# A hybrid attention block on one core: gate columns tied behind each DeltaNet recurrence, output transposes and gating issued after them

## The chip, the cores and the metric

The kernel runs as one program on one core of a Trainium2 chip. The metric is the device time in microseconds (us) of one execution. The kernel before takes 3041.43 us, the median of three runs (3039.56, 3041.43 and 3043.84). One further execution was profiled; every row shown here comes from it.

## The reference

One transformer block with a context: 1024 tokens of width 1024, 256 context tokens, 8 heads. An input projection feeds two mixers, a differential attention and a gated DeltaNet; their outputs are merged under two sigmoid gates and followed by an MLP. All is f32. The part that matters here is the DeltaNet, cut to its core:

```python
qkv = silu(depthwise_conv_centred(concat([p[3], p[4], p[5]]), conv_w))   # 7 taps
q, k, v = split(qkv);  q = l2_normalize(q) * 128**-0.5;  k = l2_normalize(k)
# per head and direction, in chunks of the sequence
t_mat = triangular_solve(eye + a_mat, eye)          # a_mat from k k^T, beta, decay
def step(state, xs):
    v_new = u_i - w_i @ state
    o_i = q_i @ state + qk_i @ v_new
    state = state * g_i + k_i^T @ v_new
out_x = rms_norm(ox_f + flip(ox_b), norm_g) * silu(z)                    # forward + backward
# later: y = sigmoid(p[11]) * (o_da @ w_br_da) + sigmoid(p[12]) * (o_dn @ w_br_dn)
```

`p[3]`, `p[4]`, `p[5]`, `p[6]` are the q, k, v and z projections of the DeltaNet, `p[11]` and `p[12]` the columns of the two merge gates, all of them products of the input with columns of one weight.

## The kernel before

**Projections.** One projection of a head makes 128 columns for 1024 tokens. The weight's eight pieces of 128 x 128 come by DMA on SyncE's queue (line 146), ScalarE casts each to a high part `whi` (149), GpSimd makes the low part `wlo` (150), and `gemm_cols` runs three matmuls to each accumulation step (`uh·whi`, `ul·whi`, `uh·wlo`, lines 164 to 166) into the PSUM tile `pg`: 8 pieces x 3 x 2 halves of 512 tokens = 48 matmuls. The q, k and v projections (`dn_proj`) are evicted into `cvraw` (429) and convolved: ScalarE makes the middle tap, VectorE six more in each of two halves (440), ScalarE the silu (442). The z projection (`dn_gate`) needs no convolution: ScalarE evicts it with silu straight into `sz` (455), of which there is one buffer.

**A head.** `dn_prep` works ahead for the next head: it transposes k (486) and q (493), takes their norms (497), makes the decays (465 to 470), the matrices `cm` (520, 523) and `pm` (528, 530), and inverts blocks of 32 by a long list of VectorE instructions in `slX`, `slY` and `slL` (540 to 582), which go to DRAM and back (`xd`, `yd`, loads at 596 and 599). `dn_pre` transposes v and k for the head itself (646, 653). `dn_double` (611 to 634) extends the inverse from 32 to 128 rows, and `dn_chain` runs the recurrence over ten chunks in both directions: per step and direction `k·S` (676), `xs` on VectorE (678), `cm·xs` (680), scalings on ScalarE (683, 686), `k·ws` (688), the new state `S` on VectorE (693), and for the eight chunks of x the outputs (698 to 707) summed in `oacc`. After the last step the head's norm is taken (712 to 719), `oacc` is transposed by TensorE (723: eight 128 x 128 transposes into two PSUM tiles `po`), VectorE multiplies by the norm weight and by `sz` (725), and SyncE stores 512 KB to `odn_d` (727).

**Fillers.** The columns of the two merge gates are 16 projections of 128 columns (`fill_setup`). `fill(n)` issues the next n of them: 48 matmuls, an eviction on ScalarE (747), a store on SyncE (748). What is left of them, and the first attention head's columns (`fill_head`), come after the last head's recurrence.

**What sets the order.** Instructions are traced in the order of the source and then scheduled in one list by the framework, from the dependencies, a model of the costs and a priority; `self.rank(...)` sets the priority of a block. The recurrence and, in this kernel, the output transposes have the first rank (`R_CHAIN` = 0), preparation and inverse follow (`R_PREP`, `R_INV`), then the convolutions (`R_CONV`). Fillers and projections take their place in source order behind these, so `ORD` decides which of them lies next to which part. Each engine then executes its own list in order. In `dn_phase` a head's recurrence is traced, then v of the next head, k and q of the one after, two sets of gate columns, and z of the next head.

Of the kernel before, what the change touches and what calls it, by code (L numbers as in the profile page):

```python
# [32 lines left out]
W2 = (5, 5)  # L33
NB = 6
BK = (1, 1, 2, 2)
ORD = 'vkqffz'
GAP = 8
SPLIT = 508
W1 = (2, 4)
# [14 lines left out]
class K:  # L54
# [602 lines left out]
    def dn_chain(self, h, r):  # L657

        nc, dw, ds = self.nc, self.dw, self.ds
        qT, kT, vtok, pm, sz, ktok, rq, b2, bdl, cm = (  # L660
            r[x] for x in ("q", "k", "vtok", "pm", "z", "ktok", "rq", "b2", "bdl", "cm"))
        ch = lambda a, c: a[:, c * P:(c + 1) * P]
        oacc = dw.tile([P, NX, P], F32, name="oacc", bufs=1)
        order = (list(range(NT)), [1, 0] + list(range(NT - 1, NC0 - 1, -1)))
# [2 lines left out]
        for step in range(NT):  # L667
            for d in range(2):
                c = order[d][step]
                last = step == NT - 1  # L670
                S0 = S[d]
                pc = self.pc.tile([P, 3, P], F32, name=f"pc{d}")
                if S0 is None:
                    xs = vtok[:, c]
                else:
                    nc.tensor.matmul(pc[:, 0], lhsT=self.ck(kT, c), rhs=S0, start=True, stop=True)
                    xs = ds.tile([P, P], F32, name=f"xs{d}", bufs=1)
                    nc.vector.scalar_tensor_tensor(out=xs, in0=pc[:, 0], scalar=self.necg[:, d, c, h:h + 1], in1=vtok[:, c],
                                                   op0=ALU.mult, op1=ALU.add)
                nc.tensor.matmul(pc[:, 1], lhsT=cm[d][:, c], rhs=xs, start=True, stop=True)  # L680
                if not last:
                    ws = ds.tile([P, P], F32, name=f"ws{d}", bufs=1)
                    nc.scalar.activation(out=ws, in_=pc[:, 1], func=AF.Copy, scale=bdl[d][:, c:c + 1])
# [33 lines left out]
        so = self.rsqrt(ds, so, NX, "so")  # L717
        nc.vector.tensor_tensor(out=so, in0=so, in1=rq, op=ALU.mult)
        nc.vector.tensor_tensor(out=oacc, in0=oacc, in1=so.unsqueeze(2).to_broadcast((P, NX, P)), op=ALU.mult)
        for q in range(2):  # L720
            pt = self.po.tile([P, 4, P], F32, name="po")
            for c in range(4):
                nc.tensor.transpose(out=pt[:, c], in_=oacc[:, 4 * q + c], identity=self.ident)
            szq = sz[:, 512 * q:512 * q + 512]
            nc.vector.scalar_tensor_tensor(out=szq, in0=pt.rearrange("p a b -> p (a b)"), scalar=self.dng, in1=szq,
                                           op0=ALU.mult, op1=ALU.mult)
# [800 lines left out]
    def dn_phase(self):  # L1527
        tc = self.tc
        R = [{} for _ in range(H + 2)]

        def proj(h, *names):
            for nm in names:
                if h < H:
                    self.dn_gate(h, R[h]) if nm == "z" else self.dn_proj(h, nm, R[h])

        proj(0, "k", "q")
        with self.rank(R_PREP):
            self.dn_prep(0, R[0])
        proj(0, "v")
        proj(1, "k", "q")  # L1540
        proj(0, "z")
        for h in range(H):
            with self.rank(R_PREP):
                self.dn_pre(h, R[h])
            if h + 1 < H:
                with self.rank(R_PREP):
                    self.dn_prep(h + 1, R[h + 1])
            with self.rank(R_CHAIN):
                self.dn_double(h, R[h])
                self.dn_chain(h, R[h])  # L1550
            if h == H - 1:
                self.fill(100)
                self.fill_head()
            for c in ORD:
                if c == "f":
                    self.fill(1)
                else:
                    proj(h + (2 if c in "kq" else 1), c)
        self.ranks_off()


# [36 lines left out]
```

## Time and profile before

| | |
|---|---|
| median of three runs | 3041.43 us |
| profiled execution | 3038.64 us (span 3036.9) |
| TensorE matmul busy | 2828.2 us (93%), 15928 matmuls |
| VectorE | 2008.3 us (66%) |
| ScalarE | 1333.1 us (44%) |
| GpSimd | 656.6 us (22%) |
| granted TensorE clock, mean | 0.958 |
| DeltaNet heads | about 320 to 1296 us |
| first attention score (line 877) | 1350.9 us |

The shares are means over stages with different limits, so the windows of a single stage say more. Matmuls overlap each other, and the listed time of one is longer than the distance to the next. In the text below a *recurrence* is the stretch from a head's first doubling matmul to its last chain matmul, a *gap* the stretch from there to the next head's first doubling matmul. Recurrences of heads 0 to 7 are, rounded: 320 to 399, 445 to 515, 578 to 646, 687 to 767, 838 to 903, 963 to 1038, 1097 to 1165 and 1211 to 1285 us.

### The profile page before, as it was taken

The numbers are of one execution on the slowest core, as the hardware profiler recorded it, in microseconds if no ns is written. First come the engines' busy times: TensorE is split into PE (matmuls) and PEld (weight loads), VectorE is DVE, ScalarE is ACT, GpSimd is POOL, SyncE is SP. The second block draws the span as 40 slices with busy tenths as digits, with TensorE's granted clock in tenths as the row PEclk, the third lists the DMA queues.
The fourth block names the chain that finished last, engine by engine and source line by source line (L and its number), as shares of the span: only waits on it lengthen the run. The fifth ranks groups of instructions, "written<-read, shape, count | busy, mean of one in ns | idle before, by whom it ended". The sixth has DMA issues, their size and how long they took to land. (4 is left out here: it accounts for less than half of the span.)

```text
span 3036.9 us, 44469 instructions
## 1 busy us (share of the span) xinstructions
PE 2828.2 (93%) x15928; PEld 2273.6 (75%) x15928; DVE 2008.3 (66%) x3675; ACT 1333.1 (44%) x3269; POOL 656.6 (22%) x756
## 2 busy tenths in 40 slices
PE   7998989899898999989999999899999999989998
PEld 4886768677686777868887778677777677768887
DVE  4768497794967767247777778664486776544435
ACT  4655244444443544326655556564465422322210
POOL 1234223532423241021111110101001643100000
PEclk9999799998998999789999999999999999999999
DMA  7631211211212122173433332416564544453321
GB/s 253 190 110 43 52 48 34 67 53 41 70 33 66 34 63 67 37 186 81 105 93 93 91 88 66 91 39 198 158 220 131 164 143 120 137 194 104 104 63 63
DMA packets 340973, 303.09 MB, mean 100 GB/s; under 512 B 87892, under 2 KB 287700, under 8 KB 339728
## 3 DMA queue, kind: packets, MB, share of 16 engines
q1 hardware_dynamic: 318864, 252.14, 28.5%
q10 hardware_dynamic: 18304, 37.41, 4.8%
q0 software_dynamic: 3584, 10.71, 1.0%
q8 instruction: 125, 2.05, 0.3%
q14 instruction: 96, 0.79, 0.1%
HBM read 212.08 MB, written 66.06 MB: 92 GB/s over the span
## 5 line engine op out<-in xcount | busy, mean ns | idle before, releaser
L150 POOL TENSOR_TENSOR wlo<-wraw,whi 128x256 fp32r<-128x256 f32 x312 | 320.7, 1033 | 1219.5 <-ACT whi L149 987.3
L164 PE MATMUL pg<-uh,whi 128*128 128x512 f32 x1152 | 481.7, 418 | 6.6 <-ACT whi L149 3.2
L166 PE MATMUL pg<-uh,wlo 128*128 128x512 f32 x1152 | 481.3, 418 | 6.1 <-POOL wlo L150 5.8
L165 PE MATMUL pg<-ul,whi 128*128 128x512 f32 x1152 | 481.4, 418 | 0.0
L149 ACT CAST whi<-wraw 128x256 fp32r<-128x256 f32 (+1 forms) x568 | 241.0, 430 | 322.9 <-PE pg L165 102.9
L166 PEld LDWEIGHTS pg<-uh,wlo 128*128 128x128 f32 x1152 | 224.6, 195 | 49.9 <-POOL wlo L150 11.1
L164 PEld LDWEIGHTS pg<-uh,whi 128*128 128x128 f32 x1152 | 224.9, 195 | 47.0 <-ACT whi L149 4.8
L165 PEld LDWEIGHTS pg<-ul,whi 128*128 128x128 f32 x1152 | 224.8, 195 | 39.6
L1370 PE MATMUL pa<-B,A 128*128 128x512 f32 x768 | 220.6, 395 | 13.6 <-ACT B L1318 5.0
L1370 PE MATMUL pg<-B,A 128*128 128x512 f32 x768 | 219.5, 393 | 0.0
L150 DVE TENSOR_TENSOR wlo<-wraw,whi 128x256 fp32r<-128x256 f32 (+1 forms) x256 | 136.6, 542 | 120.8 <-ACT whi L149 119.1
L888 DVE TENSOR_REDUCE mp<-sx 128x1 f32<-128x1024 f32 x128 | 155.7, 1218 | 49.8 <-PE sx L878 49.4
L1370 PEld LDWEIGHTS pa<-B,A 128*128 128x128 f32 x768 | 145.9, 190 | 46.9 <-ACT B L1318 5.4
L1370 PEld LDWEIGHTS pg<-B,A 128*128 128x128 f32 x768 | 146.2, 190 | 30.7
L893 ACT ACTIVATE p<-sx,mx 128x1024 f32<-128x1024 f32 x128 | 143.2, 1118 | 53.2 <-DVE mx L889 41.9
L916 PEld LDWEIGHTS pat<-V,aT 128*128 128x128 f32 x1280 | 151.0, 193 | 14.6 <-ACT aT L914 12.1
L916 PE MATMUL pat<-V,aT 128*128 128x128 f32 x1280 | 158.8, 279 | 0.0
L913 PE MATMUL pat<-ident,p 128*128 128x128 f32 x640 | 119.6, 285 | 8.0 <-ACT oh L917 5.0
L1386 DVE TENSOR_TENSOR acc<-pa,acc 128x512 f32<-128x512 f32 x32 | 22.1, 690 | 157.0 <-PE pa L1370 157.0
L1318 ACT CAST A<-araw 128x1024 fp32r<-128x1024 f32 x32 | 33.6, 1052 | 209.7 <-PE pg L1370 171.8
L913 PEld LDWEIGHTS pat<-ident,p 128*128 128x128 f32 x640 | 74.6, 142 | 56.2 <-ACT aT L914 21.3
L877 PE MATMUL sx<-K,Q 128*128 128x512 f32 x256 | 109.5, 428 | 2.9 <-DMA wraw<-in_w_in_dram 2.0
(457 smaller groups left out, 6701.8 us busy)
## 6 DMA issues: line engine op xcount, KB each, us to landing
wraw<-in_w_in_dram SPq DMA_DIRECT2D x288, 128.0 KB
wraw<-in_w_in_dram SPq DMA_DIRECT2D x64, 256.0 KB
uraw<-in_w_mlp_dram SPq DMA_DIRECT2D x32, 512.0 KB
braw<-in_w_mlp_dram SPq DMA_DIRECT2D x32, 512.0 KB
araw<-ff_d SPq DMA_DIRECT2D x32, 512.0 KB
ff_d<-ue SPq DMA_DIRECT2D x52, 256.0 KB
adraw<-in_w_ada_dram SPq DMA_DIRECT2D x32, 320.0 KB
wa<-in_w_ada_dram SPq DMA_DIRECT2D x8, 1024.0 KB
```

What stands on the lines that cost most here:

```text
L149: nc.scalar.copy(out=hi, in_=raw)
L150: self.weng.tensor_tensor(out=lo, in0=raw, in1=hi.bitcast(F32), op=ALU.subtract)
L164: nc.tensor.matmul(o, lhsT=hi, rhs=a, start=k == 0, stop=False)
L165: nc.tensor.matmul(o, lhsT=hi, rhs=b, start=False, stop=False)
L166: nc.tensor.matmul(o, lhsT=lo, rhs=a, start=False, stop=k == KT - 1)
L877: nc.tensor.matmul(ps, lhsT=Q[m][:, qs], rhs=Kh[m][:, ks], start=True, stop=False)
L888: nc.vector.tensor_reduce(out=mp[:, m, 0:1], in_=px[m], axis=AX.X, op=ALU.max)
L893: nc.scalar.activation(out=p[:, CTX:], in_=px[m], func=AF.Exp, bias=mx[:, m:m + 1], accum_out=sp[:, 0, m:m + 1])
L913: nc.tensor.transpose(out=pt[:, c], in_=a[:, (c0 + c) * P:(c0 + c + 1) * P], identity=self.ident)
L916: nc.tensor.matmul(po, lhsT=aT[:, c], rhs=r["v"][:, c], start=c == 0, stop=c == NT - 1)
L1318: nc.scalar.copy(out=z[:, 0], in_=x)
L1370: mm = lambda x, y, **kw: nc.tensor.matmul(ps[c], lhsT=a[:, x, k], rhs=bt[:, y, s], **kw)
```

## The change

`ORD` is gone. `dn_chain` ends with the normalised `oacc`; the transposes, the gating and the store stand in a function of their own, `dn_finish`, which is traced without the first rank. After a head's recurrence v of the next head and k and q of the one after are traced, then one set of gate columns whose TensorE instructions are queued behind the head's last `cm·xs` matmul (`tc.issue_after`), then `dn_finish`, then z of the next head and a second set of gate columns. For the last head `dn_finish` is traced after all that is left of the fillers. No computation is added or left out.

```diff
--- before.py
+++ after.py
@@ -33,7 +33,6 @@
 W2 = (5, 5)
 NB = 6
 BK = (1, 1, 2, 2)
-ORD = 'vkqffz'
 GAP = 8
 SPLIT = 508
 W1 = (2, 4)
@@ -657,8 +656,8 @@
     def dn_chain(self, h, r):
 
         nc, dw, ds = self.nc, self.dw, self.ds
-        qT, kT, vtok, pm, sz, ktok, rq, b2, bdl, cm = (
-            r[x] for x in ("q", "k", "vtok", "pm", "z", "ktok", "rq", "b2", "bdl", "cm"))
+        qT, kT, vtok, pm, ktok, rq, b2, bdl, cm = (
+            r[x] for x in ("q", "k", "vtok", "pm", "ktok", "rq", "b2", "bdl", "cm"))
         ch = lambda a, c: a[:, c * P:(c + 1) * P]
         oacc = dw.tile([P, NX, P], F32, name="oacc", bufs=1)
         order = (list(range(NT)), [1, 0] + list(range(NT - 1, NC0 - 1, -1)))
@@ -677,7 +676,7 @@
                     xs = ds.tile([P, P], F32, name=f"xs{d}", bufs=1)
                     nc.vector.scalar_tensor_tensor(out=xs, in0=pc[:, 0], scalar=self.necg[:, d, c, h:h + 1], in1=vtok[:, c],
                                                    op0=ALU.mult, op1=ALU.add)
-                nc.tensor.matmul(pc[:, 1], lhsT=cm[d][:, c], rhs=xs, start=True, stop=True)
+                r["end"] = nc.tensor.matmul(pc[:, 1], lhsT=cm[d][:, c], rhs=xs, start=True, stop=True)
                 if not last:
                     ws = ds.tile([P, P], F32, name=f"ws{d}", bufs=1)
                     nc.scalar.activation(out=ws, in_=pc[:, 1], func=AF.Copy, scale=bdl[d][:, c:c + 1])
@@ -717,6 +716,11 @@
         so = self.rsqrt(ds, so, NX, "so")
         nc.vector.tensor_tensor(out=so, in0=so, in1=rq, op=ALU.mult)
         nc.vector.tensor_tensor(out=oacc, in0=oacc, in1=so.unsqueeze(2).to_broadcast((P, NX, P)), op=ALU.mult)
+        r["o"] = oacc
+
+    def dn_finish(self, h, r):
+
+        nc, oacc, sz = self.nc, r["o"], r["z"]
         for q in range(2):
             pt = self.po.tile([P, 4, P], F32, name="po")
             for c in range(4):
@@ -1551,11 +1555,16 @@
             if h == H - 1:
                 self.fill(100)
                 self.fill_head()
-            for c in ORD:
-                if c == "f":
+                self.dn_finish(h, R[h])
+            else:
+                proj(h + 1, "v")
+                proj(h + 2, "k", "q")
+
+                with tc.issue_after(R[h]["end"].ins):
                     self.fill(1)
-                else:
-                    proj(h + (2 if c in "kq" else 1), c)
+                self.dn_finish(h, R[h])
+                proj(h + 1, "z")
+                self.fill(1)
         self.ranks_off()
```

In the new kernel lines up to about 718 stand one line higher (676 is 675), the output transposes are line 727, the gating 729.

TensorE in the recurrence of head 0: chain matmuls (676 to 699) and, where there are any, projection matmuls (164 to 166). Before:

```order
L676 MATMUL pc_3545<-S_3521,kT 128x128
L164 MATMUL pg<-uh,whi 128x512
L698 MATMUL po<-S_3521,qT 128x128
L688 MATMUL pc_3562<-ws_3567,ktok 128x128
L165 MATMUL pg<-ul,whi 128x512
L166 MATMUL pg<-uh,wlo 128x512
L680 MATMUL pc_3545<-xs_3547,cm 128x128
L698 MATMUL po<-S_3538,qT 128x128
L699 MATMUL po<-wp_3569,pm 128x128
L676 MATMUL pc_3596<-S_3572,kT 128x128
L164 MATMUL pg<-uh,whi 128x512
```

Now, at the same steps of that chain:

```order
L675 MATMUL pc_3596<-S_3572,kT 128x128
L675 MATMUL pc_3579<-S_3555,kT 128x128
L697 MATMUL po<-S_3555,qT 128x128
L697 MATMUL po<-S_3572,qT 128x128
L679 MATMUL pc_3579<-xs_3581,cm 128x128
L679 MATMUL pc_3596<-xs_3598,cm 128x128
L687 MATMUL pc_3579<-ws_3584,ktok 128x128
L698 MATMUL po<-wp_3586,pm 128x128
L687 MATMUL pc_3596<-ws_3601,ktok 128x128
L698 MATMUL po<-wp_3603,pm 128x128
```

The projection matmuls between the chain's matmuls are gone from here.

VectorE in the recurrence of head 4, around the same four chain steps (`xs_9054` to `xs_9088`). Before, with pieces of a convolution (440) and of the next head's inverse (565, 566) between them:

```order
L678 SCALAR_TENSOR_TENSOR xs_9054<-pc_9052,necg,vtok 128x128
L566 TENSOR_REDUCE slX<-slY 104x2
L440 SCALAR_TENSOR_TENSOR vT<-cvraw,taps,vT 128x772
L693 SCALAR_TENSOR_TENSOR S_9011<-S_8977,edec,pc_9001 128x128
L707 TENSOR_TENSOR oacc<-po,oacc 128x128
L565 TENSOR_TENSOR slY<-slX,slL 104x8
L440 SCALAR_TENSOR_TENSOR vT<-cvraw,taps,vT 128x772
L678 SCALAR_TENSOR_TENSOR xs_9037<-pc_9035,necg,vtok 128x128
L693 SCALAR_TENSOR_TENSOR S_9062<-S_9028,edec,pc_9052 128x128
L566 TENSOR_REDUCE slX<-slY 104x2x2
L440 SCALAR_TENSOR_TENSOR vT<-cvraw,taps,vT 128x772
L678 SCALAR_TENSOR_TENSOR xs_9088<-pc_9086,necg,vtok 128x128
```

Now, with evictions of `cm` (522) for the next head:

```order
L677 SCALAR_TENSOR_TENSOR xs_9054<-pc_9052,necg,vtok 128x128
L706 TENSOR_TENSOR oacc<-po,oacc 128x128
L692 SCALAR_TENSOR_TENSOR S_9011<-S_8977,edec,pc_9001 128x128
L706 TENSOR_TENSOR oacc<-po,oacc 128x128
L522 SCALAR_TENSOR_TENSOR cm<-pt,nb_8495,dec 128x128
L677 SCALAR_TENSOR_TENSOR xs_9037<-pc_9035,necg,vtok 128x128
L522 SCALAR_TENSOR_TENSOR cm<-pt,nb_8501,dec 128x128
L692 SCALAR_TENSOR_TENSOR S_9062<-S_9028,edec,pc_9052 128x128
L522 SCALAR_TENSOR_TENSOR cm<-pt,nb_8495,dec 128x128
L522 SCALAR_TENSOR_TENSOR cm<-pt,nb_8501,dec 128x128
L677 SCALAR_TENSOR_TENSOR xs_9088<-pc_9086,necg,vtok 128x128
```

The convolution and the inverse have left this stretch, the next head's `cm` has come into it.

VectorE at the end of the gap between heads 3 and 4: the copy into `z` (612, now 611) is the first VectorE instruction of head 4's doubling. Before, `cm` evictions for the following head stand ahead of it:

```order
L523 SCALAR_TENSOR_TENSOR cm<-pt,nb_8495,dec 128x128
L523 SCALAR_TENSOR_TENSOR cm<-pt,nb_8501,dec 128x128
L523 SCALAR_TENSOR_TENSOR cm<-pt,nb_8495,dec 128x128
L523 SCALAR_TENSOR_TENSOR cm<-pt,nb_8501,dec 128x128
L523 SCALAR_TENSOR_TENSOR cm<-pt,nb_8495,dec 128x128
L523 SCALAR_TENSOR_TENSOR cm<-pt,nb_8501,dec 128x128
L523 SCALAR_TENSOR_TENSOR cm<-pt,nb_8495,dec 128x128
L523 SCALAR_TENSOR_TENSOR cm<-pt,nb_8501,dec 128x128
L612 COPY z_8706<-po 32x320
L530 TENSOR_TENSOR pm<-pt,dec 128x512 x2
L612 COPY z_8706<-po 32x320
```

Now the end of a convolution and the gating of head 3 (729) do:

```order
L439 SCALAR_TENSOR_TENSOR qT<-cvraw,taps,qT 128x516
L439 SCALAR_TENSOR_TENSOR qT<-cvraw,taps,qT 128x508
L439 SCALAR_TENSOR_TENSOR qT<-cvraw,taps,qT 128x516
L439 SCALAR_TENSOR_TENSOR qT<-cvraw,taps,qT 128x508
L439 SCALAR_TENSOR_TENSOR qT<-cvraw,taps,qT 128x516 x3
L729 SCALAR_TENSOR_TENSOR sz<-po,dng,sz 128x512
L439 SCALAR_TENSOR_TENSOR qT<-cvraw,taps,qT 128x516
L611 COPY z_8706<-po 32x320
L729 SCALAR_TENSOR_TENSOR sz<-po,dng,sz 128x512
L611 COPY z_8706<-po 32x320
```

The convolution's steps have come into the gap and stand ahead of the doubling.

TensorE in the same gap. Before, the output transposes of head 3 (723) stand among projection matmuls, and the doubling of head 4 follows 149 rows further on:

```order
L165 MATMUL pg<-ul,whi 128x512
L166 MATMUL pg<-uh,wlo 128x512
L164 MATMUL pg<-uh,whi 128x512
L165 MATMUL pg<-ul,whi 128x512
L723 MATMUL po<-ident,oacc 128x128 x8
L166 MATMUL pg<-uh,wlo 128x512
L164 MATMUL pg<-uh,whi 128x512
L165 MATMUL pg<-ul,whi 128x512
L166 MATMUL pg<-uh,wlo 128x512
```

Now the transposes (727) stand three rows ahead of the doubling (610):

```order
L163 MATMUL pg<-uh,whi 128x512
L485 MATMUL pt<-ident,kT 128x128 x2
L164 MATMUL pg<-ul,whi 128x512
L165 MATMUL pg<-uh,wlo 128x512
L163 MATMUL pg<-uh,whi 128x512
L164 MATMUL pg<-ul,whi 128x512
L165 MATMUL pg<-uh,wlo 128x512
L727 MATMUL po<-ident,oacc 128x128 x8
L163 MATMUL pg<-uh,whi 128x512
L164 MATMUL pg<-ul,whi 128x512
L610 MATMUL po<-tt,cm 32x32 x10
L165 MATMUL pg<-uh,wlo 128x512
```

What stood between the transposes and the doubling stands ahead of the transposes.

## Rows read from the trace of the kernel before

**Rows 1.** The seven gaps: us, PE, PEld, DVE, ACT, POOL busy, clock, DMA

```profile
399.00:445.00 46.00, 31.71 (x136) 24.68 (x136) 45.59 (x66) 19.03 (x66) 11.96 (x14) 0.85 0.22 63
...
515.00:578.00 63.00, 51.74 (x240) 39.72 (x239) 59.37 (x105) 33.78 (x102) 34.38 (x32) 1.00 0.27 78
...
646.00:687.00 41.00, 34.76 (x159) 27.61 (x157) 37.30 (x58) 19.58 (x68) 22.07 (x15) 0.96 0.27 79
...
767.00:838.00 71.00, 60.11 (x274) 46.61 (x275) 66.41 (x124) 32.53 (x101) 32.41 (x34) 0.95 0.25 71
...
903.00:963.00 60.00, 51.87 (x248) 41.07 (x247) 52.30 (x80) 30.88 (x99) 25.28 (x31) 0.97 0.26 72
...
1038.00:1097.00 59.00, 51.99 (x240) 40.11 (x239) 51.95 (x76) 28.86 (x91) 29.88 (x26) 0.97 0.24 68
...
1165.00:1211.00 46.00, 41.36 (x186) 33.36 (x186) 41.03 (x60) 17.54 (x50) 10.89 (x13) 0.96 0.26 79
```

**Rows 2.** Windows of the recurrences of heads 0, 1, 2 and 7, same columns

```profile
320.00:399.00 79.00, 72.98 (x558) 59.49 (x558) 36.72 (x102) 27.27 (x72) 10.30 (x19) 0.78 0.19 44
...
445.00:515.00 70.00, 68.45 (x592) 57.32 (x591) 47.26 (x136) 33.52 (x90) 21.48 (x32) 0.90 0.13 28
...
578.00:646.00 68.00, 67.57 (x611) 56.48 (x610) 51.64 (x132) 29.68 (x76) 17.17 (x24) 1.00 0.15 31
...
1211.00:1285.00 74.00, 73.83 (x554) 59.34 (x554) 21.21 (x66) 23.17 (x66) 7.54 (x11) 0.77 0.16 40
```

**Rows 3.** Waits of TensorE from 340 to 1310 us: total, times, longest

```profile
PE po L723 <- DVE oacc L719: 25.8, 7, 11.0
...
PE po L611 <- DMA tt<-yd: 4.0, 2, 2.3
```

**Rows 4.** Timeline of TensorE, end of head 0's gap: start us, us, instruction

```profile
411.73 0.40 PE L165 MATMUL pg<-ul,whi 128*128 128x512 f32 x1
411.96 0.40 PE L166 MATMUL pg<-uh,wlo 128*128 128x512 f32 x1
423.35 1.97 PE L723 MATMUL po<-ident,oacc 128*128 128x128 f32 x8 [10.99 <-DVE oacc L719]
```

**Rows 5.** Windows inside two recurrences: line 676, then line 164 (PE, PEld busy)

```profile
485.00:511.00 26.00, 5.62 (x28) 4.49 (x28) 0.99 0.18 36
...
872.00:898.00 26.00, 5.19 (x26) 4.07 (x26) 1.00 0.08 22
...
485.00:511.00 26.00, 3.41 (x8) 1.53 (x8) 0.99 0.18 36
...
872.00:898.00 26.00, 6.50 (x15) 2.87 (x15) 1.00 0.08 22
```

**Rows 6.** Windows of whole recurrences, heads 1, 2 and 4, line 164 alone

```profile
445.00:515.00 70.00, 10.44 (x23) 4.66 (x23) 0.90 0.13 28
...
578.00:646.00 68.00, 15.49 (x37) 6.97 (x37) 1.00 0.15 31
...
838.00:903.00 65.00, 15.69 (x37) 6.86 (x36) 1.00 0.15 32
```

**Rows 7.** Groups of VectorE, 320 to 1296 us: busy us, mean ns, idle before

```profile
L440 DVE SCALAR_TENSOR_TENSOR vT<-cvraw,taps,vT 128x772 f32<-128x772 f32 x39 | 41.4, 1061 | 0.4 <-ACT vT L438 0.3
...
L523 DVE SCALAR_TENSOR_TENSOR cm<-pt,nb,dec 128x128 f32<-128x128 f32 x120 | 34.8, 342 | 10.2 <-PE pt L520 9.8
...
L440 DVE SCALAR_TENSOR_TENSOR qT<-cvraw,taps,qT 128x508 f32<-128x508 f32 x36 | 26.6, 739 | 0.0
...
L573 DVE TENSOR_TENSOR slY<-slX,slL 104x1024 f32<-104x1024 f32 x7 | 14.1, 2010 | 0.0
```

**Rows 8.** Waits of TensorE from 1285 to 1352 us, same columns as Rows 3

```profile
PE pg L761 <- ACT fe L758: 4.3, 2, 3.6
PE pg L164 <- ACT whi L149: 3.0, 2, 1.9
...
PE po L723 <- DVE oacc L719: 1.3, 1, 1.3
```

## The prediction

> **What bounds the kernel now.** I read the windows by stage first. From the first doubling matmul of a head to its last chain matmul I say *recurrence*, from there to the next head's first doubling matmul *gap*. In the seven gaps (386 us as windowed) VectorE is the engine that never rests: it is busy 45.6 of 46, 59.4 of 63, 37.3 of 41, 66.4 of 71, 52.3 of 60, 52.0 of 59 and 41.0 of 46 us, together 354 of 386 or 92%, while TensorE's listed time is as little as 32 of 46 [rows 1]. In the recurrences it is the other way round: TensorE is listed busy for 67.6 of 68 us in head 2, VectorE for 46 to 76% of the time in heads 0 to 2 and 29% in head 7 [rows 2]. So the two stretches have different limits, and what moves from one to the other is priced by the limit of where it lands. The waits of TensorE come next: the dearest is the output transposes waiting for the normalised `oacc`, 25.8 us in seven waits, 11.0 the longest [rows 3]; the timeline of head 0 shows that one: the last matmul starts at 411.96, the transposes at 423.35 [rows 4]. This is the wait that the change touches by name.
>
> **The tie.** It acts on TensorE only: the 48 matmuls of the gate columns that precede a head's output transposes are held behind its last `cm·xs` matmul. In head 0 it binds: nothing else that is free is left to TensorE, and its recurrence runs all but bare. In heads 1 to 6 the order shows 133 to 227 (mostly near 190) projection matmuls between the chain's end and the output transposes (before: 50 to 84), with the doubling of the next head only 1 to 20 matmuls later. Two hundred matmuls at 0.23 us, the spacing of starts in [rows 4], are 46 us, so the normalisation (11 us at most beyond what covered it) is done by then and the 25.8 us wait goes. But the end of a gap is not set by that wait where VectorE is busy throughout; what is late next is the first doubling copy on VectorE, which stands behind all of the gap's VectorE work.
>
> **What moves, counted on the two orders.** Projection and gate-column matmuls (three to an accumulation step, lines 164 to 166): inside the eight recurrences 747 before, 502 after (head 0: 94 and 4; heads 1 to 7: 653 and 498); between a chain's end and the next doubling 1131 before, 1278 after; behind the last chain 98 more. That is -245, +147 and +98, nothing lost. What now fills a recurrence are the z projection and one set of gate columns, which bring VectorE no convolution; the v, k and q projections, which bring twelve steps each shared by VectorE, lie in the gaps. VectorE's share follows: of the convolution steps 52 stood in recurrences and 5 do now, so 47 come to the gaps. Of the triangular inverse 42 pieces come to the gaps as well. The other way go 16 `cm` evictions, 52 small instructions of the next head's preparation and 3 gatings.
>
> **Recurrences (-32 us).** How much a recurrence shortens for each matmul taken out can be bounded from its late, steady part. A step in both directions leaves four records of line 676. Between 485 and 511 us there are 28 of them and 8 of line 164, so 7 steps with 24 fillers: 3.71 us a step at 3.4 fillers. Between 872 and 898 us there are 26 and 15: 6.5 steps with 45 fillers, 4.00 us at 6.9 [rows 5]. So 0.29 us for 3.5 fillers, 0.083 us each, since the step is mostly a round trip over VectorE and ScalarE. The other end is the full spacing of 0.23. Whole recurrences say even less: 69 fillers (three times 23) lasted 70 us, 111 fillers 68, another 111 only 65 [rows 2, 6]; what differs there is the granted clock, 0.90 against 1.00, and the slowest ones (0.77 and 0.78) are heads 7 and 0. I take 0.13, nearer to the row of the steady steps: 245 x 0.13 = 32 us, of which head 0 is 12. Ends: 0, by the whole recurrences, and 245 x 0.23 = 56.
>
> **Gaps (+33 us).** The 47 convolution steps cost 0.86 us each, the mean of the six groups of 224 steps, whose dearest and cheapest are 1.06 and 0.74: 40 us [rows 7]. The 42 pieces of the inverse are at most 2.0 us each, the dearest of them in [rows 7]; by the durations of the same shapes they add up to 19.5 us. Out go 16 `cm` evictions at 0.342 = 5.5 us [rows 7], the 52 small ones at about 0.3 = 15.3 us by their own shapes, and three gatings, 2.2 us. Net +37 us, 391 us of VectorE work in gaps that last 386. If no idle time at all were left, that is +5 us; if the 32 idle us stay, +37. The idle is the start of each gap (the squares of the norm on ScalarE, the evictions of the last step), and the change leaves these alone, so I keep 28 of 32: +33. The 25.8 us wait of TensorE is inside this, and is not counted again: it ran while VectorE was the busy engine.
>
> **Behind the last recurrence (+17.5 us).** The last head has no successor whose projections could hide anything: 98 more gate-column matmuls come after it and before the attention, at 0.23 us = 22.5 us. Today's stretch from 1285 to 1352 us has waits that they can fill: 4.3 us for `fe`, 3.0 for `whi`, 1.3 for the last transposes [rows 8]. I take 5 off; ends 12 to 22.5. The attention's first work is a matmul behind these on the same engine, so little else hides them.
> The Trainium skill ("Trainium Kernel Development and Optimization", Performance Expectations) says that matmul busy time misleads because matmuls are pipelined. The rows agree: starts 0.23 us apart, 0.40 listed for each [rows 4]; by the listed time the 98 would be 39 us and the total about 16 us later.
>
> **What costs nothing, and its cover.** The output transposes, the two gatings and the 512 KB store of a head are the same instructions, later in the gap. On SyncE's queue the store comes down among the loads that bring the inverse back for the doubling: in head 2 it now stands behind `xd` and `yd` and ahead of loads of `cm` and `tt`, where it stood ahead of all of them. SyncE holds those loads until the gating is done, and the doubling's second direction waits for them. Today TensorE waits twice for `tt`, 2.3 us the longer [rows 3]; that much in each of seven heads is 16 us. I cost it at 0, since VectorE ends the gap in the same places, and keep the 16 for the slow rival. `sz` has one buffer, so the z projection's activation also waits for the store, but it stands behind several of the doubling's ScalarE copies.
>
> **Sum.** -32 + 33 + 17.5 = +18.5 us on the profiled 3038.6: 3057. The median of the three runs lies 2.8 above that execution, so 3060.
>
> **Rivals.**
> *Faster: TensorE is the limit of the gaps after all.* Its matmuls are conserved, so if each one taken out of a recurrence gives back the 0.23 us that it costs elsewhere, what remains are the waits that go: 25.8 [rows 3] and 5 behind the last head, -31 us, 3010. For it: TensorE is listed at 41.4 of 46 us in the last gap, no less than VectorE there, and in the fifth gap VectorE has 8 us to spare [rows 1]. Against it: 92% there today, before 37 us are added, and the steady steps that give back 0.083, not 0.23.
> *No change:* the recurrences give back all 56 us, the gaps take 37 and the end 17.5: -1.5, 3040. It needs every filler to count in full, where head 4, with 37 groups, is shorter than head 1 with 23 [rows 6].
> *Much slower:* the recurrences give nothing back, since the emptier they are the lower the clock. Head 0's ran at a granted 0.78 with 94 fillers, head 7's at 0.77 [rows 2], so between the two levels of 1.2 and 2.4 GHz; bare ones that fall there lose what they gained. Then 0 + 37 + 22.5 = +60, 3101, and up to 16 more from the store on SyncE's queue. It decides once the clock of most recurrences is under 0.85.
> *The tie does nothing:* true of its wait in heads 1 to 6, where the matmuls would stand after the chain anyway; but the new order moves the projections in every head, so a time unchanged for this reason is ruled out.
> The Trainium skill ("Perfetto Trace Analysis", Optimization Strategy) advises interleaving regimes whose most-contended engine differs. The change does the reverse: VectorE's convolutions leave the stretches with free VectorE. By the rule the sign is the forecast's; the faster rival is the case in which it would not matter.
>
> **Chances.** Forecast (3045 to 3080) 0.53; faster rival 0.23; no change 0.14; much slower 0.10. A measurement here can tell 0.2%, 6 us. Part of the forecast's lower edge is within that: faster 0.24, same 0.16, slower 0.60. The range takes in the unknown ends of the three terms and half of the faster rival: 3020 to 3086; the forecast's own is 3045 to 3080.
>
> **What would show it.** Right: gaps 30 us longer in all with VectorE still above 90% and the copy of line 611 last; no wait at the transposes of line 727; recurrences 30 us shorter, head 0's near 67; 16 to 20 us more from the last chain matmul to the first score. Wrong: gaps no longer than 386 us in all, or recurrences that shrink by more than 50 us. The same gap length with TensorE waiting at the doubling would be the third case.

## The result and the profile after

The changed kernel takes 3114.06 us (median of four runs, 3112.20 to 3115.87) beside 3040.49 us for the kernel before: ratio 1.0246, 95% interval 1.0218 to 1.0273. That is 73.6 us slower; 18.5 us were forecast, with the right sign, and 3101 us stood as the price of the rival called much slower. The profiled execution has a span of 3110.5 us, 73.6 longer than before.

The 73.6 us lie as follows, read from the first and last matmuls of the stretches: the first doubling begins 3 us later; the eight recurrences together last 554.5 us instead of 580.1 (-25.6); the seven gaps 450.4 instead of 384.8 (+65.6); and from the last chain matmul to the end of the program 1782.0 instead of 1751.5 (+30.5). Nearly all of the gaps' growth lies in three of the seven: the third is 30 us longer, the fifth and sixth 15 and 16.

The seven gaps of the changed kernel stand here in the columns of [rows 1], with the sum of the windows as last row:

```profile
398.00:446.00 48.00, 29.59 (x135) 23.85 (x135) 43.27 (x64) 18.50 (x71) 12.48 (x19) 0.80 0.24 66
518.00:586.00 68.00, 54.71 (x238) 42.49 (x237) 58.77 (x86) 28.68 (x82) 33.56 (x22) 0.88 0.20 52
658.00:729.00 71.00, 55.34 (x246) 43.46 (x246) 61.96 (x102) 31.66 (x85) 39.86 (x27) 0.95 0.21 57
803.00:869.00 66.00, 52.94 (x226) 42.14 (x225) 56.28 (x80) 27.98 (x78) 30.80 (x22) 0.90 0.20 52
933.00:1007.00 74.00, 60.59 (x266) 48.31 (x265) 62.69 (x102) 29.89 (x85) 37.68 (x26) 0.91 0.20 54
1072.00:1147.00 75.00, 61.61 (x272) 48.74 (x270) 59.80 (x88) 35.34 (x105) 27.86 (x30) 0.89 0.23 60
1204.00:1251.00 47.00, 39.14 (x168) 30.75 (x167) 42.24 (x64) 15.75 (x45) 21.19 (x12) 0.95 0.28 76
sum 449.00, PE 353.91 PEld 279.74 DVE 385.00 ACT 187.80 POOL 203.43; mean PE 50.56 PEld 39.96 DVE 55.00 ACT 26.83 POOL 29.06
```

VectorE is busy for 385 us, close to the 391 forecast, but that is 86% of the gaps, where [rows 1] had 92%: its idle time has grown from 32 to 64 us. TensorE's busy time has grown by 30 us as well (from 324, the sum of [rows 1]), and so has the time in which it waits. Counted from the start and end of every instruction in the gaps, both engines are busy together for 309 us (295 before), TensorE alone for 47 (27), VectorE alone for 78 (57) and neither for 17 (5): each got more work, and little of it ran beside the other's. TensorE's granted clock is lower: the time at half speed (1.2 GHz instead of 2.4), twice one minus the granted share times the length, was some 35 us by [rows 1] and is 90 us here.

TensorE waits between 340 and 1310 us for the following, in the columns of [rows 3]:

```profile
PE pt L645 <- ACT vT L441: 29.5, 5, 9.1
PE pg L165 <- POOL wlo L149: 26.9, 10, 7.1
PE pt L492 <- ACT qT L441: 13.4, 1, 13.4
PE pt L485 <- ACT sq L488: 12.6, 2, 7.9
PE pt L485 <- ACT kT L441: 10.0, 3, 4.1
```

The 25.8 us at the output transposes [rows 3] are gone, as the tie and the late transposes had it. In their place stand three waits for a silu that ends a convolution (v, q and k: 52.9 us), one for the norms behind them, and one for the low weight parts from GpSimd. Before, the v and q waits were 5.1 and 5.9 us and the one for `wlo` 5.1.

The fifth gap shows the pair at work. TensorE comes first, with its waits in brackets:

```profile
973.24 1.97 PE L645 MATMUL pt<-ident,vT 128*128 128x128 f32 x8 [4.73 <-ACT vT L441]
...
993.72 0.79 PE L165 MATMUL pg<-uh,wlo 128*128 128x512 f32 x1 [7.14 <-POOL wlo L149]
994.31 0.63 PE L163 MATMUL pg<-uh,whi 128*128 128x512 f32 x1
994.74 0.63 PE L164 MATMUL pg<-ul,whi 128*128 128x512 f32 x1
```

Then comes VectorE, which stands idle a little later for what that projection brings:

```profile
997.05 5.82 DVE L439 SCALAR_TENSOR_TENSOR qT<-cvraw,taps,qT 128x516 f32<-128x516 f32 x7 [3.97 <-ACT qT L437]
1006.48 1.41 DVE L729 SCALAR_TENSOR_TENSOR sz<-po,dng,sz 128x512 f32<-128x512 f32 x2 [3.62 <-PE po L727]
```

TensorE waits for a convolution and for a weight part, runs on at half speed (0.43 us from start to start instead of 0.23), and VectorE then waits for the projection (by way of ScalarE's middle tap) and for the transposes behind it.

### The profile page after: what moved, and what is told of

It reads as the page before. It is cut to its first block, busy times and chain, and to the rows that moved or that the text cites. A ratio compares the mean times of both kernels' runs of the same rounds, so it can differ in the third digit from the quotient of the medians.

```text
span 3110.5 us, 44521 instructions
## 1 busy us (share of the span) xinstructions
PE 2844.6 (91%) x15928; PEld 2297.3 (74%) x15928; DVE 2003.4 (64%) x3675; ACT 1343.0 (43%) x3273; POOL 699.2 (22%) x756
## 5 line engine op out<-in xcount | busy, mean ns | idle before, releaser
L149 POOL TENSOR_TENSOR wlo<-wraw,whi 128x256 fp32r<-128x256 f32 x312 | 369.1, 1188 | 1177.2 <-ACT whi L148 946.0
L918 ACT COPY aT<-pat 128x384 f32<-128x384 f32 (+1 forms) x192 | 78.3, 408 | 82.5 <-PE pat L917 80.2
```

Of the source, the lines that this page charges most:

```text
L149: self.weng.tensor_tensor(out=lo, in0=raw, in1=hi.bitcast(F32), op=ALU.subtract)
```

## The experiments

All runs below stand beside runs of the kernel before on the same chip (medians 3032 to 3044 us). The theories and rivals go by the letters that the expectations give them; theory A says of each run that the convolutions pushed into the gaps, and VectorE with them, cost the time.

**Single parts of the change.** The first run leaves the tie out:

```diff
-                with tc.issue_after(R[h]["end"].ins):
-                    self.fill(1)
+                self.fill(1)
```


> The changed kernel with the first set of gate columns traced plainly, not tied behind the recurrence. By the order head 0's recurrence gets 93 projection matmuls again, but only 9 VectorE convolution steps lie in the recurrences (before 52, changed kernel 5). Theory A (the convolutions pushed out of the recurrences by the late output transposes with z behind them cost the time): 3095 to 3105, head 0's share alone comes back. Theory B (the tie costs the time): 3040 to 3055. Theory C (the last head, whose transposes now stand behind all remaining gate columns, costs it): 3114 as the changed kernel.

Measured 1.0179 (1.0142 to 1.0217) times before, 3089.8 us. The tie is worth some 20 us here, and 55 us are left without it: theory A, a little below its range. The gaps stay as long as in the change (453 us); the recurrences are 24 us shorter than the change's, 531 us.

The next run gives the finish of every head, the last one's too, its rank back and traces it directly behind the recurrence; the tie and the earlier z stay:

```diff
+                with self.rank(R_CHAIN):
+                    self.dn_finish(h, R[h])
                 proj(h + 1, "v")
 ...
-                self.dn_finish(h, R[h])
```


> The changed kernel with the finish of every head (transposes, gating, store) given back the first rank and traced directly after its recurrence; tie and earlier z stay. By the order 54 convolution steps lie in the recurrences again. Theory A: 3045 to 3065, what is left being head 0's bare recurrence under the tie. Theory B: 3100 to 3114. Theory C: about 3080, since the last head is undone with the others.

Measured 1.0019 (0.9984 to 1.0054): no difference that can be told. The gaps last 391 us, 7 more than before, with 56 convolution steps in the recurrences by the trace (57 before), though the gaps hold 112 projection matmuls more than before (1236 beside 1124). So 112 matmuls more cost the gaps 7 us as long as the convolutions are not added to them. Theory B falls.

Then z of the next head stands behind the second set of gate columns:

```diff
-                proj(h + 1, "z")
                 self.fill(1)
+                proj(h + 1, "z")
```


> The changed kernel with z of the next head behind the second set of gate columns, as before the change; tie and late finish stay. By the order 24 convolution steps lie in the recurrences, half way. Theory A: half way too, 3070 to 3090. Theory B: 3105 to 3120. Theory C: 3105 to 3120.

Measured 1.0058 (1.0035 to 1.0080), 19 us above before: less than half of the loss, below theory A's range. The gaps last 415 us.

Then the last head's finish alone is undone:

```diff
+                with self.rank(R_CHAIN):
+                    self.dn_finish(h, R[h])
                 self.fill(100)
                 self.fill_head()
-                self.dn_finish(h, R[h])
```


> The changed kernel with only the last head's finish back in the first rank, ahead of the remaining gate columns; heads 0 to 6 as changed. By the order nothing moves before the last recurrence ends. Theory A: 3105 to 3114. Theory B: 3114. Theory C: about 3080, the 34 us by which the stretch from the last chain matmul to the first score has grown come back.

Measured 1.0260 (1.0214 to 1.0307): nothing comes back that can be told. The first score starts at 1404.6 us instead of 1428.1; counted from the last chain matmul it comes 17.7 us earlier, and what follows it takes 17.4 us longer. Theory C falls; the last stretch holds the same work in another order.

**One part alone, on the kernel before.** The diffs are against the changed kernel; where the finish has its rank back, the last head's has it too. The first run keeps the late finish alone, without the tie and with z last:

```diff
-                with tc.issue_after(R[h]["end"].ins):
-                    self.fill(1)
+                self.fill(1)
                 self.dn_finish(h, R[h])
-                proj(h + 1, "z")
                 self.fill(1)
+                proj(h + 1, "z")
```


> Late finish alone: transposes, gating and store unranked behind the first set of gate columns (for the last head behind all of them), no tie, z last as before the change. By the order 56 convolution steps lie in the recurrences (before 52). Theory A (time follows the number of convolution steps that lie in the gaps, about 1.4 us each): within 10 us of before. Rival D (the late transposes cost by themselves, since gating, store and z wait for them): 20 to 40 us above before.

The second keeps the earlier z alone:

```diff
+                with self.rank(R_CHAIN):
+                    self.dn_finish(h, R[h])
                 proj(h + 1, "v")
                 proj(h + 2, "k", "q")
-                with tc.issue_after(R[h]["end"].ins):
-                    self.fill(1)
+                self.fill(1)
-                self.dn_finish(h, R[h])
                 proj(h + 1, "z")
                 self.fill(1)
```


> Earlier z alone: order v, k, q, gate columns, z, gate columns, no tie, finish ranked and directly behind the recurrence as before the change. By the order 54 convolution steps in the recurrences. Theory A: within 10 us of before. Rival E (the earlier z costs by itself, because it holds the one buffer sz or the PSUM tiles): 20 us or more above.

The third keeps the tie alone:

```diff
+                with self.rank(R_CHAIN):
+                    self.dn_finish(h, R[h])
                 proj(h + 1, "v")
                 proj(h + 2, "k", "q")
                 with tc.issue_after(R[h]["end"].ins):
                     self.fill(1)
-                self.dn_finish(h, R[h])
-                proj(h + 1, "z")
                 self.fill(1)
+                proj(h + 1, "z")
```


> The tie alone: the first set of gate columns tied behind the recurrence, finish ranked as before, z last. By the order 62 convolution steps in the recurrences; head 0's recurrence has 4 projection matmuls instead of 94. Theory A: 5 to 15 us above before, the 90 matmuls that head 0 no longer hides (90 x 0.23 = 21 us) less what its recurrence shortens (79 to 72 us in the runs so far). Rival B (the tie costs in every head): 40 us or more above.

Measured 1.0091 (1.0058 to 1.0125), 1.0071 (1.0043 to 1.0099) and 1.0059 (1.0029 to 1.0088): 28, 20 and 22 us above before. Theory A allowed 10 for the first two and 5 to 15 for the tie, and misses all three, where rivals D (20 to 40) and E (20 or more) have the late finish and the earlier z within their ranges; rival B (40 or more) falls. So each part costs something by itself, though 54 to 62 convolution steps lie in the recurrences. With the late finish alone and with the tie alone the gaps are 405 us; for the earlier z they are 389, and its profiled execution was the fastest of its ten, so where its 20 us lie stays open. Their sum, 70, is near the loss, yet they don't add: undoing the late finish alone (e_rank) removes nearly all.

**Early transposes, convolutions still in the gaps.** Here the finish stands behind the v projection, without rank but for the last head's:

```diff
                 proj(h + 1, "v")
+                self.dn_finish(h, R[h])
                 proj(h + 2, "k", "q")
 ...
-                self.dn_finish(h, R[h])
```


> Order v, finish, k, q, tied gate columns, z, gate columns; the last head's finish ranked. By the order the transposes come as early as before the change (58 to 85 projection matmuls behind the chain in heads 0 to 6), but only 10 convolution steps lie in the recurrences. Theory A: slow like the changed kernel, 50 to 75 us above before. Rival D (the late transposes, with z, the store and the gating waiting for them, make the loss): 10 to 30 above.

Measured 1.0266 (1.0233 to 1.0299), 79 us above before, with gaps of 452 us and recurrences as long as before (578 us). The transposes are as early as before, and it is as slow as the change, with the convolutions in the gaps. Late transposes (rival D, 10 to 30 here) are not needed for the loss. TensorE's longest waits in it are:

```profile
PE pg L165 <- POOL wlo L149: 40.7, 11, 9.7
PE po L727 <- DVE oacc L718: 18.0, 4, 6.6
PE pt L492 <- ACT qT L441: 13.4, 1, 13.4
```

The wait at the transposes is back at 18 us, and the total is no longer than without it. The next run has the finish first, without rank, no tie and z last:

```diff
+                self.dn_finish(h, R[h])
                 proj(h + 1, "v")
                 proj(h + 2, "k", "q")
-                with tc.issue_after(R[h]["end"].ins):
-                    self.fill(1)
-                self.dn_finish(h, R[h])
-                proj(h + 1, "z")
+                self.fill(1)
                 self.fill(1)
+                proj(h + 1, "z")
```


> Order finish (unranked), v, k, q, two sets of gate columns, z, no tie; for the last head the finish stands behind the remaining gate columns. By the order 66 convolution steps in the recurrences and 773 projection matmuls (before 52 and 747), the most of all. Theory A: as fast as before or up to 20 us faster. Rival D: within 10 us of before as well, so this run is the test for a faster version rather than between the two.

Measured 1.0028 (1.0006 to 1.0050): 12 us slower by the medians, no faster version, although of the orders so far it leaves the fewest matmuls (1105) and convolution steps (153) to the gaps. These gaps still last 414 us, 29 more than before, and those of the late finish alone 405 with 164 steps by the trace (166 before). So the length of the gaps does not follow the number of convolution steps alone; a finish without rank lengthens them by 20 to 29 us with no convolution added, and why is not shown.

**GpSimd's queue.** TensorE's wait for `wlo` had grown to 26.9 us, so the zeroings and the DMA into `cvraw`, which share GpSimd's list with it, are moved away:

```diff
-        nc.gpsimd.memset(raw[:, XO - GAP:XO], 0.0)
+        nc.vector.memset(raw[:, XO - GAP:XO], 0.0)
 ...
-            nc.gpsimd.dma_start(out=raw[:, 3:3 + CTX], ...)
+            nc.scalar.dma_start(out=raw[:, 3:3 + CTX], ...)
```


> The changed kernel with the three zeroings of cvraw moved from GpSimd to VectorE and the context DMA into cvraw from GpSimd's queue to ScalarE's. Order nearly the same: 2 convolution steps in the recurrences. Theory P (in the gaps GpSimd stands at cvraw's zeroing until VectorE has finished an older convolution, 54 us in the changed kernel's waits, and the low weight parts behind it hold TensorE for 26.9 us): 15 to 28 us less than the changed kernel, so 46 to 60 above before. Theory W (VectorE's work alone sets the gap): no less than the changed kernel, up to 5 more for the zeroings on VectorE.

Measured 1.0135 (1.0093 to 1.0178), 42 us above before and so about 32 below the change. The size is a little beyond theory P's 15 to 28, and the place is another: the gaps are 443 us, only 7 shorter, the recurrences 15 and the start 7. TensorE's wait for `wlo` is still 17.6 us. So the same edit is made to the kernel before:

> The kernel before with the zeroings of cvraw on VectorE and the context DMA into it on ScalarE's queue, as x_pool did to the changed kernel; 62 convolution steps in the recurrences (before 52). Theory P (GpSimd at the zeroings holds the low weight parts): TensorE waits only 5.1 us for these here, so at most that is gained in the gaps; x_pool's first recurrence began 6.6 us earlier, which would come here too: 3020 to 3035 beside a before of 3033 to 3040. Theory W: no change.

Measured 0.9945 (0.9920 to 0.9971), 3024.6 us: 13 us faster than the kernel before, the only faster version with all of its work. The gain comes in the recurrences (542.6 us in all instead of 580.1), not in the gaps (392), and the time at half speed in them is lower (51 us instead of 133); why is not shown.

**Less VectorE work.** Four of the six VectorE steps of each convolution half are left out, in both kernels:

```diff
-                for j in (0, 1, 2, 4, 5, 6):
+                for j in (2, 4):
```


> Control for the next run: the kernel before with four of the six VectorE steps of every convolution half left out (taps 0, 1, 5 and 6), so its output is not the block's. By the order 51 convolution steps are left in the gaps (167 before). Theory A (VectorE sets the gaps): gaps 30 to 60 us shorter in all, 2970 to 3010. Rival F (TensorE sets them): gaps no more than 15 us shorter.

> The changed kernel with the same four steps left out of every convolution half; 67 convolution steps in the gaps (214 changed). Theory A (the convolutions in the gaps, and TensorE waiting for them, make the loss): at most 30 us above the cut kernel before, against 74 uncut. Rival F (the loss is in matmuls that moved behind the recurrences, the bare recurrences and the clock): 55 us or more above it.

Measured 0.9899 (0.9863 to 0.9934), 3006.3 us, and 1.0035 (1.0015 to 1.0054), 3048.2 us. The difference between the two is 42 us instead of 74, between what theory A and rival F had said. By stages it is not the convolutions in the gaps that make it smaller: between the two cut kernels the gaps still grow by 62.5 us (377.5 to 440.0; uncut 65.6) and the recurrences shrink by 22 (uncut 26), but the stretch behind the last recurrence grows by 6 instead of 30, where the cut kernel before has 80 projection matmuls more than the uncut one (1225 by the trace, 1145 uncut). These are the gaps of the cut kernel before, then of the cut changed kernel:

```profile
sum 377.00, PE 324.33 PEld 257.81 DVE 284.67 ACT 169.07 POOL 128.58; mean PE 46.33 PEld 36.83 DVE 40.67 ACT 24.15 POOL 18.37
sum 441.00, PE 373.70 PEld 291.98 DVE 292.77 ACT 221.09 POOL 162.10; mean PE 53.39 PEld 41.71 DVE 41.82 ACT 31.58 POOL 23.16
```

In the changed kernel 92 us of VectorE work less make the gaps 8 us shorter, though the scheduler moved other work in, 20 us of TensorE's. In the kernel before, where VectorE was busy for 92% and TensorE's busy time in them is the same, 69 us less make them 7 us shorter (384.8 to 377.5). The prediction had VectorE's work as the limit of the gaps; by itself it is not, in either kernel. With VectorE's steps cut, the change lengthens the gaps mostly by time in which TensorE works alone: 136 us instead of 89.

**Less TensorE work.** One set of gate columns a head is taken out of the gaps and left over for the end, in both kernels:

```diff
-                with tc.issue_after(R[h]["end"].ins):
-                    self.fill(1)
```


> The changed kernel with the tied set of gate columns of each head not issued there but left over for the stretch behind the last recurrence (nothing is left out). By the order the gaps hold 933 projection matmuls (changed kernel 1278) and 190 convolution steps (214). Rival F (TensorE's own matmuls set the gaps): the seven gaps fall from 450 to about 370 us in all (345 x 0.23 less), the end grows by about as much, total within 25 us of the changed kernel. Theory A (VectorE's work sets them): gaps no shorter than 420 us, since 24 steps x 0.86 = 21 us are all that VectorE loses; total 30 us or more above the changed kernel.

```diff
-ORD = 'vkqffz'
+ORD = 'vkqfz'
```


> The same in the kernel before: one set of gate columns a head instead of two, the other sets left over for the end. By the order the gaps hold 921 projection matmuls (before 1131) and 178 convolution steps (167). Rival F: gaps from 385 to about 337 us. Theory A: gaps 385 to 395 us.

Measured 1.0361 (1.0329 to 1.0393), 3151.2 us, and 1.0095 (1.0062 to 1.0127), 3069.6 us: what leaves the gaps is paid behind the last recurrence. These are the gaps of the changed kernel without the set:

```profile
sum 425.00, PE 299.91 PEld 232.94 DVE 376.17 ACT 180.82 POOL 173.15; mean PE 42.84 PEld 33.28 DVE 53.74 ACT 25.83 POOL 24.73
```

345 matmuls, 79 us at 0.23, are gone and the gaps are 25 us shorter: rival F, by which TensorE alone sets them, is wrong too, and theory A's "no shorter than 420" holds. In the kernel before they fall from 385 to 358 us, where neither had it. Then both edits are made to the changed kernel together:

> The changed kernel with both relieved: the tied gate columns left over for the end (as y_late_after) and four of six VectorE steps of every convolution half left out (as x_cut_after; the output is not the block's). By the order 954 projection matmuls (1278 changed) and 60 convolution steps (214) in the gaps. Alone the two took 25 and 10 us from the gaps' 450. Theory G (TensorE and VectorE wait in turn, and the relief of one is hidden by the other): together clearly more than 35 us, gaps 330 to 390. Rival H (a third thing of fixed length, the inverse with its trips through DRAM or the norm, sets the gaps): 410 us or more.

```profile
sum 339.00, PE 281.14 PEld 221.56 DVE 275.88 ACT 166.87 POOL 120.71; mean PE 40.16 PEld 31.65 DVE 39.41 ACT 23.84 POOL 17.24
```

Measured 0.9919 (0.9893 to 0.9946), 3017.7 us, with work left out. The gaps are 339 us: 111 less, where the two edits alone gave 10 and 25. Theory G's range holds and rival H falls. TensorE and VectorE limit the gaps together; what one is relieved of, the other still holds.

## Why the prediction went as it did

**The sign and what moves** were right: the projections and convolutions moved from recurrences to gaps, the transposes' wait of 25.8 us went, and nothing was won by it. Of the 55 us that the sum is short, the gaps are 33, the stretch behind the last recurrence 13, the recurrences 6 and the later start 3.

**Recurrences, -32 forecast:** -25.6 us were measured, or 0.104 for each of the 245 matmuls, between the two bounds and near the chosen 0.13. That it came so near is partly luck, since no price per matmul set it: e_notie has 90 matmuls more in its recurrences than the change (600 by the trace, 510), and they are 24 us shorter, with some 100 us at half speed instead of 150. Head 0's bare recurrence lasts 74.1 us instead of about 67, at a granted clock of 0.68:

```profile
323.00:398.00 75.00, 61.82 (x474) 51.05 (x473) 35.91 (x102) 24.32 (x66) 4.80 (x11) 0.68 0.12 25
446.00:518.00 72.00, 70.77 (x568) 59.70 (x566) 36.60 (x128) 28.93 (x73) 17.94 (x24) 0.78 0.13 31
...
1251.00:1328.00 77.00, 74.31 (x547) 61.20 (x547) 21.21 (x66) 25.21 (x71) 6.20 (x9) 0.72 0.10 27
```

Against [rows 2] the clock of heads 0, 1 and 7 is lower (0.78, 0.90 and 0.77 there). The other five stand at 0.92 to 1.00. So a part of the "much slower" rival came true: the clock is under 0.85 in three of eight recurrences (two of which were so before), not in most.

**Gaps, +33 forecast: this is the step that failed.** +65.6 us were measured, above the term's own end of +37. The prediction priced the moved work by one limit ("VectorE is the engine that never rests"), put the 147 matmuls that came to the same gaps, 34 us at 0.23, at nothing, and kept 28 of VectorE's 32 idle us. VectorE's work was sized well: 391 us forecast, 385 measured. Its idle time was not: 64 us.

Behind that stands a misreading of the trace. The idle time was said to be the start of each gap. In the kernel before, 30 of the 32 us lie in the last tenth of the gaps, and 19 of them are the first doubling copy on VectorE waiting for TensorE's doubling matmuls, in five of the seven gaps:

```profile
688.24 0.48 DVE L612 COPY z<-po 32x320 f32<-32x320 f32 x1 [4.76 <-PE po L611]
...
1097.70 0.48 DVE L612 COPY z<-po 32x320 f32<-32x320 f32 x1 [7.50 <-PE po L611]
```

So in these five it was TensorE, listed busy for 84% of the gaps, that was late at the end, and VectorE with its 92% was idle by then. x_cut_before shows the same from the other side: a fifth of VectorE's work in these gaps gone, and they are 7 us shorter.

What the runs show in its place are two limits of about equal height. What is added to TensorE alone costs little (e_rank: 112 matmuls, 7 us; no run adds to VectorE alone), what is taken from one alone gives little (10 of 92 us, 25 of 79), and what is taken from both gives 111. Work of the two laid end to end would have shown each relief nearly in full, so that is not it. The change added to both, 30 us each as windowed, and the gaps grew by twice that, since both engines' idle time grew by 32 us as well: the convolution waits for the projection, and the transposes of v, k and q and what follows wait for the convolution. e_rank, without the added convolutions, is as fast as before; e_finv, with them, is as slow as the change. How the 32 us divide into these waits, the lower clock and the finish without rank is not shown.

**Behind the last recurrence, +17.5 forecast:** +30.5 us were measured to the end of the program, above the term's own end of 22.5, and +34 to the first score, where 16 to 20 stood as the sign of being right. The 98 matmuls are 22.5 us; the waits that were to take 5 us off did not. The rest is not taken apart: the time at half clock behind the last recurrence is 16 us longer in this trace (79 against 63), which at 0.43 instead of 0.23 us a matmul would be some 7 us.

**The rival that the tie does nothing** was ruled out rightly; e_notie puts it at some 20 of the 74 us. The wait for `tt` behind the store on SyncE's queue, up to 16 us, does not appear among TensorE's waits.

## What to carry to other kernels

A high busy share of one engine does not say that the other's share is free. Where two engines are nearly equally full and hand results to each other, as here, moved work that comes to both has to be priced in both, and by their hand-overs too. Before pricing by the fuller engine, look at which engine waits for which at the end of the stretch: an engine that is 92% busy and idle at the end is not what ends it. And a wait of 26 us that ends inside a stretch whose end is set elsewhere can be worth nothing.

## What the hardware showed that was not expected

GpSimd's low weight part (`wlo`, 128x256) can be much slower beside a busy VectorE. Three of them took 13.49 us in the fifth gap (3.40, 9.44 and 0.72 one by one), while VectorE ran steps of convolutions and of the inverse without a pause until 993.09; the one of 9.44 us ended 0.57 us after that:

```profile
980.86 13.49 POOL L149 TENSOR_TENSOR wlo<-wraw,whi 128x256 fp32r<-128x256 f32 x3 [8.78 <-ACT whi L148]
...
996.46 0.74 POOL L149 TENSOR_TENSOR wlo<-wraw,whi 128x256 fp32r<-128x256 f32 x1 [2.11 <-ACT whi L148]
```

Over 320 to 1330 us its mean is 1173 ns before, 1498 ns in the changed kernel, and 915 ns in the changed kernel with the convolutions cut. Those with VectorE idle beside them took 0.71 to 0.75 us in all three. The changed kernel:

```profile
L149 POOL TENSOR_TENSOR wlo<-wraw,whi 128x256 fp32r<-128x256 f32 x152 | 226.8, 1498 | 399.9 <-ACT whi L148 285.4 <-PE pg L165 43.4 <-ACT wp L685 38.8
```

With the convolutions cut:

```profile
L149 POOL TENSOR_TENSOR wlo<-wraw,whi 128x256 fp32r<-128x256 f32 x170 | 155.0, 915 | 463.5 <-ACT whi L148 331.1 <-PE pg L163 35.6 <-PE pg L165 34.4
```

TensorE's wait for `wlo` goes with it: 5.1 us before, 26.9 in the changed kernel and 1.4 with the convolutions cut. So packing VectorE's steps into the gaps also slowed the weights of the projections that were to fill them; what that is worth in time is not shown. The Trainium skill ("GPSIMD Engine Reference", 1. Specifications) says that GpSimd shares its SBUF interfaces with VectorE and contends with VectorE instructions that have two SBUF inputs; a convolution step is one (`cvraw` and its own accumulator). The trace agrees in direction: 0.74 us alone, 3.40 and 9.44 beside them.
